# A squared-ReLU MLP on TensorE: the up projection of parts two to four as seven half-size products per tile pair

## The chip, the cores and the metric

The kernel runs on one core of a Trainium2 chip. The metric is the device time of one execution in microseconds. Three runs of the kernel before took 1084.81 to 1085.42 us, median 1085.13. A separate profiled execution took 1085.44 us, of which 1083.7 us lie between its first and its last instruction (the span).

## The reference, cut to what matters

One layer of a hybrid encoder on 512 tokens of width 1024, in float32: a combined input projection, a bidirectional state-space branch, a windowed attention branch, a gated merge and an output projection, then the channel mixing that this change is about:

```python
h = rmsnorm(x, pre_mlp_norm)                       # 512 x 1024
f = jnp.square(jax.nn.relu(h @ w_mlp_in)) @ w_mlp_out   # 1024 -> 4096 -> 1024
x = x + rmsnorm(f, post_mlp_norm)
```

## The kernel before, in words

**Float32 as two float32r numbers.** TensorE multiplies `float32r` operands. Each operand X is split into a high part (a cast on ACT) and a low part (X minus the high part, on POOL or DVE), and a product is three matmuls into one PSUM bank: high x high, high x low, low x high (`mm3`, lines 404 to 408; all matmuls show as line 398). Weights are the stationary operand in the up projection and the moving one in the down projection.

**Quanta.** The program is a list of quanta: each names the weight chunks that it needs and a function that issues its matmuls. `prefetch` (481) loads chunks ahead on SP's queue into three buffers `wr` (line 453) and splits them into three pairs `wh`, `wl`: ACT casts (473), and the letters of a string say which engine subtracts which piece (477; "pppp" is four quarters on POOL, "v" stands for DVE). A list of actions is placed at quantum numbers (`at`); all that is issued inside `held_back` (1341) may not be put ahead of the TensorE instruction issued last before it.

**The order of the work.** The instructions are not run in the order in which they are written. `Planner` (77) knows a cost per instruction and simulates the engines; each engine takes the ready instruction with the earliest due time, except TensorE, which takes the first ready one in program order. `chain` (498) then fixes one order for each engine, SP's queue of DMA issues included. On the chip each engine runs its list strictly in that order.

**The MLP.** The 4096 hidden columns are four parts of 1024, and a part is eight tiles of 128 columns, taken as four pairs (tile n and tile n + 4). An up quantum (`up_quantum`, 1491) is one such tile: 8 blocks of 128 x 3 matmuls, 512 tokens wide, 24 matmuls into one bank `pp`, then ReLU and square (`up_done`, 1441; ACT line 1446, DVE line 1449). After each second tile `combine` (1457) makes from the pair the token-side operands of the down projection.

The down projection of a part is a 2 x 2 block product of tokens and columns, done in the Winograd form of Strassen's scheme: seven products instead of eight, from four sums of the token-side operand (S1 to S4) and four of the weights (T1 to T4). `down_quanta` (1604) lists them and `fold` (1522) issues them: a quantum is one product, 24 matmuls of 512 columns. The T sums are made on DVE (lines 1536, 1537) from the raw weights `wd`, or, where `staged` is given, read ready from DRAM; the split of a down weight is line 1571 (ACT) and 1575 (POOL, or DVE by `LO_DOWN`). `done` (1616) adds a finished bank to the token accumulators `acc` (1621).

Each down quantum of part p is followed by an up quantum of part p + 1. The first three tiles of the first part are split by token halves (`up_halves`), so that they can begin before all tokens have come through the norm: `flip_h2` (1422) transposes the normed tokens on TensorE and splits them into the tiles `b`, called `h2` in the code. The first use of staged sums is `stage_wo` (1347) with `mix_quanta` (1366), for the output projection ahead of the MLP.

## Time and profile before

| | before |
|---|---|
| median of three runs | 1085.13 us (1084.81 to 1085.42) |
| profiled execution: its time, its span | 1085.44 us, 1083.7 us |
| TensorE matmuls: busy, count | 1073.5 us (99%), 5584 |
| DVE busy | 785.1 us (72%) |
| ACT busy | 654.4 us (60%) |
| POOL busy | 808.1 us (75%) |
| bytes moved by DMA | 152.21 MB |
| TensorE clock granted | 0.997 of full speed |

How to read it: the span is cut by engine. PE is TensorE's matmuls, PEld its weight loads, which overlap the matmuls. Matmul durations in the profile contain their pipelined end, so their mean is longer than their distance; the distance of two matmuls in a stretch without holes is the price. The chain of waits follows the last instruction back to what released it. Waits on an engine that is not on that chain cost nothing by themselves. `L1536` in a row is line 1536 of the kernel, and `wt<-wd,wd` are its output and inputs by the program's names.

### The profile page before, as it was taken

Reading aid. Unit: us, or ns where it says so; the run is one execution under the profiler, and the core shown is the slowest. Engines: PE = TensorE matmul, PEld = TensorE weight load, DVE = VectorE, ACT = ScalarE, POOL = GpSimd, SP = SyncE. Lnnn points to the kernel's source line nnn. Section 1 sums busy time; section 2 is a strip of 40 time slices with the busy share of each in tenths; the row PEclk is TensorE's granted clock in tenths of the full one; section 3 lists DMA queues with packets and bytes.
Section 4 is the critical chain, followed back from the end, with each engine's and each line's share of the span. In section 5 each row is a group of like instructions: output and inputs, shape, how many; then the busy total and the mean of one; then the engine's idle time right before and its main releaser. Section 6 shows DMA issues by size and latency. Waiting matters only on the chain.

```text
span 1083.7 us, 16956 instructions
## 1 busy us (share of the span) xinstructions
PE 1073.5 (99%) x5584; PEld 902.2 (83%) x5584; DVE 785.1 (72%) x1345; ACT 654.4 (60%) x1407; POOL 808.1 (75%) x1011
## 2 busy tenths in 40 slices
PE   9999999999999999999999999999999999999997
PEld 8888888888888888888888888889888888888885
DVE  6578787788796787887877558668873755755787
ACT  5566776686865767676686522476755434434443
POOL 4446567557558898989898768566998978978844
PEclk9999999999999999999999999999999999999999
DMA  7444624625536555556564389754722612611522
GB/s 218 118 121 125 150 76 123 146 74 158 131 107 164 149 144 160 158 143 167 136 179 113 103 253 332 226 198 127 237 65 59 201 53 59 198 55 59 161 93 78
DMA packets 221000, 152.21 MB, mean 140 GB/s; under 512 B 12493, under 2 KB 194229, under 8 KB 220912
## 3 DMA queue, kind: packets, MB, share of 16 engines
q1 hardware_dynamic: 220764, 151.06, 48.6%
q8 instruction: 44, 0.72, 0.3%
q14 instruction: 44, 0.36, 0.1%
q10 hardware_dynamic: 148, 0.07, 0.0%
HBM read 138.19 MB, written 12.91 MB: 139 GB/s over the span
## 4 chain that ended last, share of the span: by engine, by line
PE 94%; DVE 2%; DMA 2%; ACT 1%; SPq 1%; issue 1%; POOL 0%; POOLq 0%; DVEq 0%
PE pp L398 66%; PE ps L398 25%; PE ps L402 3%; DMA x<-in_x 1%; DMA wr<-in_w_in 0%; ACT b L423 0%; DVE B L944 0%; DVE x L1401 0%; DVE P L855 0%; DVE x L1655 0%; DVE acc L1621 0%; SPq L383 0%; SPq L570 0%; DVE Q L832 0%; DVE ag L1648 0%
## 5 line engine op out<-in xcount | busy, mean ns | idle before, releaser
L398 PE MATMUL pp<-b,wh 128*128 128x512 f32 (+1 forms) x1840 | 564.8, 388 | 0.2 <-DVE b L424 0.2
L477 POOL TENSOR_TENSOR wl<-wr,wh 128x256 fp32r<-128x256 f32 (+1 forms) x503 | 418.2, 860 | 137.4 <-ACT wh L473 133.9
L398 PEld LDWEIGHTS pp<-b,wh 128*128 128x128 f32 x1840 | 340.2, 188 | 68.2 <-issue 1.5
L398 PE MATMUL pp<-b,wl 128*128 128x512 f32 (+1 forms) x920 | 356.5, 388 | 0.0
L398 PEld LDWEIGHTS pp<-b,wl 128*128 128x128 f32 x920 | 172.9, 188 | 34.3
L473 ACT CAST wh<-wr 128x1024 fp32r<-128x1024 f32 x131 | 136.5, 1042 | 82.0 <-PE pp L398 56.1
L1575 POOL TENSOR_TENSOR wl<-wd,wh 128x256 fp32r<-128x256 f32 x168 | 139.8, 862 | 39.9 <-ACT wh L1571 31.9
L1571 ACT CAST wh<-wd 128x512 fp32r<-128x512 f32 x108 | 63.2, 618 | 53.9 <-PE pp L398 23.8
L398 PE MATMUL ps<-wh,fh 128*128 128x512 f32 (+1 forms) x196 | 75.5, 385 | 0.5 <-DVE acc L1621 0.5
L398 PE MATMUL ps<-wl,fh 128*128 128x512 f32 (+1 forms) x196 | 75.5, 385 | 0.0
L398 PE MATMUL ps<-wh,fl 128*128 128x512 f32 (+1 forms) x196 | 75.4, 385 | 0.0
L1112 ACT ACTIVATE n<-cb,tables 128x128 f32<-128x128 f32 x128 | 48.8, 391 | 26.8 <-DVE cb L1103 22.8
L1449 DVE SCALAR_TENSOR_TENSOR pp<-pp,r 128x512 f32<-128x512 f32 (+1 forms) x31 | 17.5, 565 | 54.0 <-ACT r L1446 53.9
L1575 POOL TENSOR_TENSOR wl<-wt,wh 128x256 fp32r<-128x256 f32 x56 | 45.4, 844 | 9.9 <-ACT wh L1571 6.0
L944 DVE SCALAR_TENSOR_TENSOR u<-pp,cv,u 128x510 f32<-128x510 f32 (+1 forms) x64 | 47.6, 744 | 2.9 <-ACT u L940 1.7
L1042 POOL TENSOR_TENSOR xd<-x,tables 128x256 f32<-128x256 f32 x48 | 35.0, 747 | 19.5 <-ACT x L967 16.9
L1113 ACT ACTIVATE m<-cb,tables 128x128 f32<-128x128 f32 x128 | 48.7, 389 | 0.3 <-DVE cb L1103 0.3
L1148 POOL TENSOR_TENSOR w<-w,E 128x256 f32<-128x256 f32 x48 | 40.3, 852 | 11.1 <-DVE w L1144 5.4
L398 PEld LDWEIGHTS ps<-wh,fh 128*128 128x128 f32 x196 | 36.8, 188 | 8.1 <-DVE acc L1621 0.7
L1108 ACT ACTIVATE rf<-rf,tables 128x128 f32<-128x128 f32 x128 | 41.9, 393 | 2.6 <-DMA rf<-csT 2.6
L398 PEld LDWEIGHTS ps<-wl,fh 128*128 128x128 f32 x196 | 36.8, 188 | 7.4
L398 PEld LDWEIGHTS ps<-wh,fl 128*128 128x128 f32 x196 | 36.8, 188 | 7.2
(301 smaller groups left out, 2085.3 us busy)
## 6 DMA issues: line engine op xcount, KB each, us to landing
wr<-in_w_in SPq DMA_DIRECT2D x74, 512.0 KB, 4.8
wr<-in_w_mlp_in SPq DMA_DIRECT2D x32, 512.0 KB, 4.1
wd<-in_w_mlp_out SPq DMA_DIRECT2D x64, 256.0 KB, 4.7
rb<-csT SPq DMA_DIRECT2D x32, 256.0 KB, 3.9
rf<-csT SPq DMA_DIRECT2D x32, 256.0 KB, 5.5
wr<-in_w_ssd_out SPq DMA_DIRECT2D x14, 512.0 KB, 5.4
wd<-in_w_o SPq DMA_DIRECT2D x28, 256.0 KB, 4.6
E<-csE SPq DMA_DIRECT2D x96, 64.0 KB, 3.9
```

The lines of the kernel that those rows point to most:

```text
L398: self.nc.tensor.matmul(out, lhsT, rhs, start=start, stop=stop, skip_group_check=more)
L402: self.nc.tensor.transpose(out, src, self.ident[:n, :n])
L473: self.nc.scalar.copy(hi[:, :m], raw)
L477: engines[e].tensor_tensor(lo[:, c], raw[:, c], hi[:, c].bitcast(F32), op=ALU.subtract)
L944: nc.vector.scalar_tensor_tensor(u[:, a:e], ps[:, a + d:e + d], self.wtap(t, b), u[:, a:e], op0=ALU.mult, op1=ALU.add)
L1042: nc.gpsimd.tensor_tensor(v4(xd[:, d * 256:(d + 1) * 256]), v4(xs(c)), by_dir(self.coef, c)[:, d].unsqueeze(2).to_broadcast([128, 4, 64]), ...
L1108: nc.scalar.activation(v4(rf)[:, h], v4(rf)[:, h], AF.Identity, bias=ncs[:, 0, h:h + 1])
L1112: nc.scalar.activation(v4(n)[:, h], cb[:, 0], AF.Copy, scale=dt[:, 0, h:h + 1])
L1113: nc.scalar.activation(v4(m)[:, h], cb[:, 1], AF.Copy, scale=dt[:, 1, h:h + 1])
L1148: nc.gpsimd.tensor_tensor(wc, wc, E[:, d], op=ALU.add)
L1571: nc.scalar.copy(hi, w)
L1575: (nc.vector if e == "v" else nc.gpsimd).tensor_tensor(low[:, q], w[:, q], hi[:, q].bitcast(F32), op=ALU.subtract)
```

## The change

The up projection of parts two to four takes the same seven-product form. Its 2 x 2 blocks are halves of the input width (512 rows of `w_mlp_in`), halves of a part's columns, and halves of the tokens (256). For a tile pair there are seven products of 4 blocks x 3 matmuls, 256 tokens wide, in four quanta of two products, the last of one (`one`, `two`, `three`, `four`); they are accumulated in the halves of two banks, X and V in one, Z and Y in the other. ACT copies intermediate banks out (`copy`), DVE adds them back (`plus`), and ReLU and square go by quarters (`square`, which takes the minimum side where a block is held with its sign turned). Part one keeps the old form.

The token-side sums T1 to T4 are made once, after the tokens have been transposed: `flip_h2` also writes a float32 copy of them (`b32`, 16 more ACT operations), `token_sums` makes T1, T2, T4 on DVE with their splits, and `third_sum` splits T3 at the start of part one's down projection.

The weight-side sums S1 to S4 of parts two to four are made by DMA alone, in DRAM: a copy on SP's queue, then an accumulating DMA issued by POOL (`sums_in_dram`), eight transfers of 512 x 512 for each part, at quanta 10, 26 and 42 with two quanta between. In the same way the down sums T1 to T4 of parts three and four are made from 4 and 30 quanta after the start of the up projection on, three quanta between, and read as staged. [...]

A tile pair needs 3.5 chunks of 1024 weight columns instead of 2. Two quarters of each full chunk are subtracted on DVE ("vvpp"), the half chunk on POOL. A quarter of the down splits of parts two and three moves from POOL to DVE ("pppv"). The planner learns costs for DMAs issued by POOL, and counts other transfers as 1.6 times as long while one of them runs. The slots of SBUF grow from 67 to 73, and the scratch for POOL's DMAs is set to 4096.

```diff
-SLOTS, RAW, SPL, PP, AHEAD, SPARE = 67, 3, 3, 3, 4, 6
+SLOTS, RAW, SPL, PP, AHEAD, SPARE = 73, 3, 3, 3, 4, 6
+UP_LO = "vvpp", "vvpp", "vvpp", "pp"
-LO_DOWN = "p", "p", "p", "vp"
+LO_DOWN = "p", "pppv","pppv","vp"
+SOFT, SLOW = 125, 1.6
-FETCH, STAGE = 2, 1
+FETCH, STAGE, HALF = 2, 1, 3
+SUMS = dict(up={1: (10, 2), 2: (26, 2), 3: (42, 2)}, down={2:(104,3),3:(130,3)})
...
             if e == "SP":
-                queue = max(queue, t + self.LEAD) + self.transfer(n)
+                queue = max(queue, t + self.LEAD)
+                queue += self.transfer(n) * (SLOW if queue < soft else 1)
...
+            elif e == "POOL" and "DMA" in type(self.ins[n]).__name__:
+                size = 4 * math.prod(d[1] for d in self.operands(self.ins[n].outs)[0].ap)
+                soft = max(soft, end + self.LEAD) + size / SOFT
+                free[e], end = end, soft + self.TAIL
...
+    def sums_in_dram(self, name, src, q, pace):
+        nc = self.nc
+        t = [self.dp.tile([512, 512], F32, name=f"{name}s{i}") for i in range(1, 5)]
+        def step(out, a, plus):
+            def run():
+                a_ = t[a] if isinstance(a, int) else src(*a)
+                if plus:
+                    nc.gpsimd.dma_start(t[out], a_, accum_op=ALU.add)
+                else:
+                    nc.sync.dma_start(t[out], a_)
+            return run
+        steps = [(0, (0, 0), False), (0, (0, 1), True), (2, (0, 1), False), (2, (1, 1), True),
+                 (1, 0, False), (1, (1, 1), True), (3, 1, False), (3, (1, 0), True)]
+        for i, args in enumerate(steps):
+            self.at(q + pace * i, lambda fn=step(*args): self.held_back(fn))
+        return t
...
+                if t2 == 0:
+                    self.b32.append(self.slots.get("b32"))
+                nc.scalar.activation(self.b32[k + i][:, tok], ps[:, i * 256:(i + 1) * 256], AF.Copy, scale=self.g3(k + i))
...
+    def token_sums(self):
...
+        for k in range(4):
+            b1, b2 = self.b32[k], self.b32[4 + k]
...
+            tt(u[:, lo], b1[:, lo], b1[:, hi], op=ALU.subtract)
+            stt(u[:, hi], u[:, lo], -1.0, b2[:, hi], op0=ALU.mult, op1=ALU.subtract)
+            self.split(h, l, u)
...
+            tt(self.t3[-1][:, half], b2[:, hi], b1[:, hi], op=ALU.subtract)
+            stt(four[-1][:, half], u[:, hi], -1.0, b2[:, lo], op0=ALU.mult, op1=ALU.subtract)
...
+            if k % 2:
+                h, l = self.twin("t4")
+                self.split(h, l, four[-1])
...
+    def up_unit(self, part, k):
...
+        def product(w, b, at, first):
+            ps, cols = bank[at[0]], at[1]
+            for i in range(4):
+                self.mm3(ps[:, cols], (w[0][:, i], w[1][:, i]), self.bt[b][i], first and i == 0, i == 3, not first)
+        def copy(n, at):
+            made[n] = get(n, (128, 256))
+            nc.scalar.copy(made[n], bank[at[0]][:, at[1]])
+        def plus(at, a, n):
+            nc.vector.tensor_tensor(bank[at[0]][:, at[1]], bank[a[0]][:, a[1]], made[n], op=ALU.add)
+            put(made.pop(n))
+        def square(at, r, side, dst=None):
+            a, cols = bank[at[0]], at[1]
+            nc.scalar.activation(r[:, cols], a[:, cols], AF.Relu, scale=1.0 if side == ALU.max else -1.0)
+            nc.vector.scalar_tensor_tensor((dst or a)[:, cols], a[:, cols], 0.0, r[:, cols], op0=side, op1=ALU.mult)
...
+        X, Y, Z, V = (1, lo), (0, hi), (0, lo), (1, hi)
+        def one(w):
+            bank[1] = self.bank("pp")
+            product(w[0], "B11", X, True)
+            copy("c0", X)
+            bank[0] = self.bank("pp")
+            product(w[1], "T1", Y, True)
+            copy("cy", Y)
+        def two(w):
+            product(w[0], "T2", X, False)
+            copy("c1", X)
+            product(w[1], "B21", Z, False)
+            plus(Z, Z, "c0")
+            made["r"] = get("r")
+            square(Z, made["r"], ALU.max)
+            self.operand(part, k, bank[0][:, lo])
+        def three(w):
+            product(w[0], "T3", X, False)
+            plus(V, X, "cy")
+            square(V, get("q"), ALU.min)
+            product(w[1], "B22", Y, False)
+            plus(Y, Y, "c1")
+            square(Y, made["r"], ALU.max, made["r"])
+        def four(w):
+            product(w[0], "T4", X, False)
+            square(X, get("q"), ALU.min)
+            self.pair = [bank[0][:, lo], made["r"][:, hi], made["r"], bank[1]]
+            self.combine(part, k, -1.0)
...
+        return [quantum(("A11", "S1"), one, UP_LO[0]), quantum(("S2", "A12"), two, UP_LO[1]),
+                quantum(("S3", "S4"), three, UP_LO[2]), quantum(("A22",), four, UP_LO[3])]
...
+            if part == 0:
+                self.at(n(), self.third_sum)
+            up = [u for k in range(4) for u in self.up_unit(part + 1, k)] if part < 3 else []
             for i in range(8):
-                self.add(*down[i:i + 1], *([self.up_quantum(8 * part + 8 + i)] if part < 3 else []))
+                self.add(*down[i:i + 1], *up[2 * i:2 * i + 2])
```

So after each of the first seven down quanta two of a pair's four quanta follow, and after the seventh the last two follow directly on the two before them.

177 lines of the change are left out of this document (137 added, 40 removed).

## The prediction

> **What bounds the kernel now.** First the page, then the chain of waits, the waits of TensorE and of the SP queue, and the busy times of stages.
>
> ```profile
> span 1083.7 us, 16956 instructions
> PE 1073.5 (99%) x5584; PEld 902.2 (83%) x5584; DVE 785.1 (72%) x1345; ACT 654.4 (60%) x1407; POOL 808.1 (75%) x1011
> ```
>
> A TensorE that is busy for 99% may still have slack inside its modelled durations, so the pitch of its matmuls is read from the chain (start us, us, what):
>
> ```profile
> 757.96 4.80 PE pp L398 x40
> 762.76 2.40 PE ps L398 x20
> 765.16 21.79 PE pp L398 x96
> 787.40 5.44 PE pp L398 x24
> ...
> 797.83 5.44 PE pp L398 x24
> 803.27 5.44 PE ps L398 x24
> ...
> 1026.31 10.88 PE pp L398 x48
> 1037.19 32.65 PE ps L398 x144
> ```
>
> From 765 us on the pieces follow each other without a hole: 24 matmuls of 512 columns take 5.44 us, 226.7 ns each. The 60 before them belong to the split first tiles, 256 columns wide: 4.80 + 2.40 = 7.20 us, 120.0 ns each. So half the width costs 53% of the full width here, and the weight load that goes with each matmul does not show at that pitch.
>
> ```profile
> PE ps L398 <- DVE acc L1621: 0.5, 1, 0.5
> PE pp L398 <- DVE b L424: 0.2, 1, 0.2
> ```
>
> Those are TensorE's waits outside the start. TensorE alone sets the time, and only fewer matmul nanoseconds, or a new wait, can change it. How near the others are to becoming the bound is read by stage:
>
> ```profile
> core 0: us, PE busy (x) PEld busy (x) DVE busy (x) ACT busy (x) POOL busy (x), PEclk, DMA share, GB/s
> 766.00:787.40 21.40, 21.40 (x96) 17.74 (x95) 17.84 (x36) 14.23 (x31) 21.08 (x33) 1.00 0.82 252
> 787.40:795.00 7.60, 7.60 (x36) 6.28 (x35) 6.50 (x9) 4.02 (x8) 7.60 (x9) 1.00 0.04 13
> 795.00:805.00 10.00, 10.00 (x46) 8.29 (x45) 8.87 (x12) 5.17 (x9) 9.70 (x18) 1.00 0.19 54
> 787.40:869.00 81.60, 81.60 (x362) 67.60 (x361) 49.59 (x75) 41.61 (x74) 75.87 (x102) 1.00 0.35 105
> 869.00:950.60 81.60, 81.60 (x362) 67.59 (x361) 49.17 (x78) 37.18 (x65) 70.64 (x90) 1.00 0.35 104
> 950.60:1037.20 86.60, 86.60 (x384) 71.74 (x383) 54.23 (x88) 38.67 (x69) 69.01 (x85) 1.00 0.29 89
> 200.00:300.00 100.00, 100.00 (x617) 84.91 (x616) 78.98 (x170) 73.54 (x184) 63.63 (x83) 1.00 0.48 125
> ```
>
> The rows from 787.4 on are the stages in which down part one, two, three runs with up part two, three, four between. POOL is the second bound (93% in the first of them), DVE has some 30 us of room in each, but almost none between 766 and 805.
>
> **The change part by part.** *TensorE.* A tile pair of parts two to four was 48 matmuls of 512 columns, 2 x 5.44 = 10.88 us; it becomes 7 products x 4 blocks x 3 = 84 of 256 columns, 84 x 120.0 ns = 10.08 us. Twelve pairs x 0.80 = **9.60 us removed**. Nothing else on TensorE changes.
>
> *Bank hand-overs inside a pair.* Seven products share two PSUM banks, and copies, additions and squares lie between them. The costs:
>
> ```profile
> L415 ACT CAST fh<-pp 128x256 fp32r<-128x256 f32 x8 | 3.0, 373 | 7.2 <-DVE r L1449 4.7 <-DVE pp L1449 2.6
> L1449 DVE SCALAR_TENSOR_TENSOR pp<-pp,r 128x256 f32<-128x256 f32 x4 | 1.7, 425 | 6.2 <-ACT r L1446 6.2
> L1449 DVE SCALAR_TENSOR_TENSOR pp<-pp,r 128x512 f32<-128x512 f32 x4 | 2.8, 696 | 11.9 <-ACT r L1446 11.9
> ```
>
> Before the last product (T4) the third (T3) must be added and squared: addition 0.42, relu 0.37, square 0.43 = 1.22 us, under the B22 product, 12 x 120 ns = 1.44 us. That leaves 0.22 us for three semaphore hand-overs, so some wait is likely there unless a down product is put in between. Between the second and third quantum of a pair a down product (5.44 us) covers the longer chain (2.0 us), except in the fourth pair of each part, where no down product is left. Bounds: 0, or 12 x 0.2 + 3 x 1.2 = 6.0 us. A planner that puts the first matmuls of the next ready product there removes most of it; I take 1.0.
>
> *Splits of weights.* 3.5 chunks of 1024 columns per pair instead of 2. POOL keeps its eight quarter pieces per pair; the six new ones go to DVE, and ACT casts 1.5 chunks more.
>
> ```profile
> L477 POOL TENSOR_TENSOR wl<-wr,wh x503: 713/742/2408, 21.6 to 1024.7; 128x256 fp32r<-128x256 f32 x167, 128x1024 fp32r<-128x1024 f32 x1
> L477 DVE TENSOR_TENSOR wl<-wr,wh x6: 410/950/964, 740.9 to 745.7; 128x256 fp32r<-128x256 f32 x6
> L477 DVE TENSOR_TENSOR wl<-wr,wh 128x256 fp32r<-128x256 f32 x6 | 4.3, 774 | 0.0
> L1575 DVE TENSOR_TENSOR wl<-wd,wh x24: 679/692/1232, 669.2 to 1065.0; 128x512 fp32r<-128x512 f32 x24
> L416 DVE TENSOR_TENSOR fl<-fs,fh x16: 682/993/1359, 770.3 to 1042.6; 128x512 fp32r<-128x512 f32 x16
> L473 ACT CAST wh<-wr 128x1024 fp32r<-128x1024 f32 x8 | 8.4, 1051 | 8.1 <-PE pp L398 6.5 <-DMA wd<-in_w_mlp_out 0.7 <-PE ps L398 0.3
> ```
>
> The second row is the price that decides: the same DVE subtraction takes 0.41 us or 0.95 us. The short ones fall where POOL is pausing, the long ones beside POOL's subtractions. The Trainium skill ("SBUF — State Buffer", section "Who interferes with whom" and its practical consequences) says that a DVE instruction with two SBUF inputs and a GpSimd instruction that reads SBUF block each other for the whole instruction. The two values of the row agree with it; by that rule nearly all the new splits would cost the long price, which is the second rival below.
>
> ACT gets per part at most 4 x (1.5 x 1.05 + 3 copies x 0.37 + 4 relus x 0.37) = 17 us on 37 to 42 of 78: nothing, covered by its idle time; without that cover DVE, which waits for each cast, would be late by as much. DVE per part: 24 d for the splits (d between 0.41 and 0.95), 8 additions x 0.42 = 3.4, and 16 squares of 0.425 for 4 x 0.70 + 8 x 0.425, 0.6 more. A quarter of the down splits of parts two and three also moves to it, 7 x 0.83 = 5.8 us a part (bounds 0.68 to 1.23).
>
> *Token sums.* Per block pair four operations of 256 columns and one split subtraction of 512, and two more splits per four: 4 x (4 x 0.41 + 0.68) + 2 x 0.68 = 10.6 us of DVE, or at the long prices 4 x (4 x 0.95 + 1.36) + 2 x 1.36 = 23.4; I take 15. They are wanted from 794 us on. From 766 to 805 DVE is idle 3.6 + 1.1 + 1.1 = 5.8 us. So some 9 us are pushed behind 805 us; what is late next is the down weights' sums on DVE, operands of products that TensorE wants in the same stretch. Bounds: 0 (later DVE work gives way, as after 805 the first stage is only 61% busy), or the full 9; I take 2.0.
>
> *Stages one and two as a whole.* DVE needs 49.6 + 49.2 + 48 d + 2 x 4.0 + 5.8 + 2.0 (the third token sum) + 7 carried over = 121.6 + 48 d, and TensorE would leave 2 x 78.4 = 156.8 us. DVE is the bound above d = 0.73. I take d = 0.74, near the mean of the six rows (0.77), as POOL works less in the second stage (14 pieces x 0.83 = 11.6 us less): 0.3 us, and 1.0 for queueing of an engine that is then 100% planned. In stage three the staged down sums remove 16 sums from DVE,
>
> ```profile
> L1536 DVE TENSOR_TENSOR wt<-wd,wd 128x512 f32<-128x512 f32 x8 | 8.0, 996 | 1.5 <-POOL wl L1575 0.8 <-DMA wd<-in_w_mlp_out 0.7
> L1536 DVE TENSOR_TENSOR wd<-wd,wd 128x512 f32<-128x512 f32 x4 | 4.6, 1158 | 5.8 <-DMA wd<-in_w_mlp_out 5.8
> L1537 DVE TENSOR_TENSOR wd<-wd,wd 128x512 f32<-128x512 f32 x4 | 4.4, 1096 | 0.0
> ```
>
> 17.0 us, so its full 3.2 us arrives. That relief itself gains nothing, since TensorE waits for nothing there now.
>
> *Sums in DRAM.* Five sets of eight 1 MB transfers: 20 copies on SP's queue, 20 accumulating ones issued by POOL, and 15 MB more weight loads.
>
> ```profile
> q1 hardware_dynamic: 220764, 151.06, 48.6%
> wr<-in_w_mlp_in SPq DMA_DIRECT2D x32, 512.0 KB, 4.1
> wot<-wd SPq DMA_DIRECT2D x16, 256.0 KB, 4.7
> SPq L453 <- POOL wl L477: 261.5, 96, 7.2
> ```
>
> No row shows an accumulating transfer. At the queue's own rate (151 MB in 48.6% of 1083.7 us, 287 GB/s) 1 MB takes 3.7 us; reading twice and writing once, three times that, 11 us. Three sets run up to quantum 57, about the first 330 us at 5.4 us a quantum and a little more, where the DMA engines are 48% busy and POOL 64%; two run from the up projection on. A weight load is issued as soon as POOL frees its buffer, three buffers deep, about two quanta (10.9 us) before it is wanted, and takes 4.1: some 6.8 us late is free. A single transfer of 3.7 to 11 us ahead of it is thus hidden or nearly so. The Trainium skill ("DMA: Bandwidth & Descriptors", "Anatomy of one DMA") gives a GpSimd-issued transfer about 2.0 us plus bytes over 436 GB/s, an estimate of 4.4 us for 1 MB, and the sum would be the same. POOL's own issue cost is bounded by its shortest and longest work rows, 0.2 and 2.4 us; eight fall where POOL would be at 75.9 of 78.4, yet they can slide into the second stage, as their readers come later still. Bounds 0 and 4; I take 0.8 for all of this.
>
> **Sum**, on the profiled execution's 1085.44 us: -9.6 + 1.0 + 2.0 + 1.3 + 0.8 = -4.5, 1080.9. It stood 0.3 above the median of the runs, so **1080.6 us**.
>
> **The rivals.** (1) *All cover holds*: the planner's order hides every hand-over; -9.6, with 0.6 of unavoidable edges: 1076. For it: today TensorE waits 0.7 us in the whole second half though POOL is 93% busy. Against: DVE's 766 to 805. (2) *DVE becomes the bound*: every new split costs 0.95 beside POOL, and the seven moved ones 1.23 (2.8 more): 121.6 + 45.6 + 2.8 = 170.0 against 156.8, 13.2 lost for 9.6 won, +3.6: 1088.7. It eats the whole gain from d = 0.93. For it: four of the six rows are at 0.95. Against: the 512-wide splits of the down weights have median 0.69. (3) *SP's queue stands behind a sum*: in each set two copies read an accumulated block, so SP waits for POOL's transfer, and every weight load stands behind it. The copy comes three steps (33 us) after the accumulation. If that takes 45 us (a twelfth of the rate above), each blocks 12 us, 5.2 more than a load can be late: ten copies, +52 less 9.6, 1127. Against: that is four times the upper bound. (4) *The hand-overs cost their upper bound*, 6.0 instead of 1.0, because the order finds nothing to put between: 1085.6, no change. Against: the planner puts the first ready matmul next. (5) *It does not do what it says*: a 256-column stream paced by its weight loads. The rows at 120.0 ns exclude all but 1%.
>
> **How the numbers follow.** Forecast (1078 to 1083) 0.42, (1) 0.22, (4) 0.13, (2) 0.15, (3) with (5) 0.08. About 0.2% (2.2 us) is what a measurement of this kernel can tell from no change: faster, below 1083, is the forecast, (1) and the near edge of (4), 0.66; within 0.2% most of (4) and the near edge of (2), 0.13; slower the rest, 0.21. The range 1075.3 to 1089 takes in (1) and most of (2); (3) and the far end of (2) stay out.
>
> **What would show it.** The chain should still be TensorE's, a pair of parts two to four taking 10.1 us and a stage 78.4 to 80. The new DVE splits should have a mean near 0.74; above 0.93 the second rival holds. TensorE's waits should name DVE between 790 and 830 us, and the PSUM operations of the pairs. SP's waits should name no accumulating transfer for more than 7 us. I am wrong if stage three too is over 80 us, or if TensorE waits in the first 600 us.

## The result, and the profile after

The changed kernel takes 1102.73 us (median of 4 runs, 1099.62 to 1104.93) against 1085.28 us for the kernel before beside it. The ratio is 1.0157, 95% interval 1.0129 to 1.0185: 1.6% slower, where 1080.6 us had been predicted, with a range up to 1089.0.

The page of the changed kernel: engines, the two large DMA queues, and the chain that ended last.

```profile
span 1101.6 us, 18311 instructions
PE 1074.3 (98%) x6016; PEld 915.6 (83%) x6016; DVE 838.7 (76%) x1471; ACT 695.3 (63%) x1515; POOL 814.4 (74%) x1003
...
q1 hardware_dynamic: 249212, 187.77, 58.5%
q0 software_dynamic: 10560, 20.97, 11.6%
...
PE 61%; DVE 9%; DMA 3%; ACT 3%; issue 2%; SPq 1%; POOL 0%; POOLq 0%; DVEq 0%; ACTq 0%
```

TensorE now holds only 61% of the chain. The new queue q0 holds the accumulating transfers: 20.97 MB, whose packets took 11.6% of the time of 16 DMA engines over 1101.6 us. For each of the 20 transfers that is 127.8 / 20 = 6.4 us of all 16 engines, added up over the engines; it does not show that all were busy with it at once.

To see where the time went, both executions are cut at the same piece of work, ahead of the last 1316 matmuls before and the last 1750 after (the difference is the 432 that the change adds). The first part reaches into the up projection of part one, the second holds the down stages with the new products. Stretches, before and then after; columns: us, busy us and count of TensorE, weight loads, DVE, ACT, POOL, then clock, DMA share, GB/s.

```profile
0.00:779.80 779.80, 777.59 (x4270) 656.91 (x4271) 587.96 (x1029) 514.35 (x1153) 563.98 (x704) 1.00 0.56 157
779.80:1076.00 296.20, 295.69 (x1316) 245.24 (x1314) 193.35 (x310) 139.52 (x252) 243.10 (x307) 1.00 0.32 96
```

```profile
0.00:790.90 790.90, 780.91 (x4268) 656.02 (x4269) 589.93 (x1036) 519.38 (x1170) 575.47 (x713) 1.00 0.70 186
790.90:1093.90 303.00, 293.19 (x1750) 259.60 (x1748) 245.02 (x428) 175.36 (x343) 237.99 (x290) 0.99 0.73 203
```

The first part, in which TensorE's work is unchanged, is **11.1 us later**. The second takes 303.0 us. With the predicted 9.6 us less work it would take 296.2 - 9.6 = 286.6 if nothing new were waited for, so **16.4 us are lost in it**. The sum, 11.1 - 9.6 + 16.4 = 17.9, is the difference of the spans, 1101.6 - 1083.7. Not all of it is seen as waiting. Idle time of TensorE (length less busy time) is 7.8 us more than before in the first part and 9.3 more in the second; the rest, 3.3 and 7.1 us, lies in matmuls that took longer than before or than priced. A slower clock after a wait is one cause (0.73 in a row below); holes that the modelled durations hide are another, since the timeline gives 0.39 us to a matmul of 512 columns whose pitch is 0.227.

The saving itself is there, by a row of the chain (start us, us, what):

```profile
1002.87 5.75 PE pp L412 x48
```

48 half-width matmuls take 5.75 us, 119.8 ns each, as priced. TensorE's longest waits (us in all, times, longest):

```profile
PE ps L416 <- DVE P L893: 5.0, 4, 3.3
PE pp L412 <- DVE fal L430: 2.5, 3, 1.2
PE pp L412 <- DVE pp L1573: 2.2, 2, 1.2
```

The first is in the scan steps, far ahead of the new products, and the kernel before does not have it: `P` are attention weights, which DVE makes in one queue with the scan's row blocks. The three stages, each from the first matmul of a part's down products to that of the next part's:

```profile
803.80:885.10 81.30, 78.69 (x481) 70.54 (x480) 70.93 (x110) 50.26 (x95) 72.50 (x87) 0.98 0.64 179
885.10:969.10 84.00, 80.78 (x506) 71.55 (x505) 69.62 (x125) 47.13 (x92) 69.59 (x81) 1.00 0.94 242
969.10:1051.90 82.80, 79.38 (x506) 71.78 (x505) 59.60 (x112) 49.64 (x97) 60.22 (x74) 1.00 0.69 204
```

The stages take 81.3, 84.0 and 82.8 us instead of 78.4. The first holds 24 up matmuls fewer than the others, which run behind its end.

**The scan steps.** Stretches at TensorE's largest hole in the first half:

```profile
290.00:300.00 10.00, 9.36 (x43) 7.41 (x41) 2.08 (x3) 6.18 (x21) 2.27 (x3) 1.00 0.77 169
300.00:310.00 10.00, 5.84 (x21) 4.22 (x22) 9.96 (x23) 6.86 (x16) 8.37 (x10) 0.73 0.59 193
```

The issue of an accumulating transfer on POOL and then of a row block `rf` of the scan on SP (start us, us of issue), and that of the row block in the kernel before:

```profile
278.91 0.99 POOL L1460 DMA_DIRECT2D up2s<-in_w_mlp_in  x1
...
284.14 1.66 SPq L1110 DMA_DIRECT2D rf<-csT  x1
```

```profile
289.57 0.55 SPq L1087 DMA_DIRECT2D rf<-csT  x1
```

The row block is issued 5.2 us behind the accumulating transfer, in 1.66 us instead of 0.55, and its landing is then on the chain:

```profile
284.14 9.66 DMA rf<-csT
```

Over all 32 of these loads the median to landing rose from 5.5 to 6.8 us. DVE starves first (2.08 of 10 us busy from 290), then TensorE waits for it. The accumulating transfers' issue on POOL (ns: min, median, max; first and last start) and their us to landing:

```profile
L1460 POOL DMA_DIRECT2D up2s<-in_w_mlp_in x4: 989/1033/1113, 215.0 to 324.8; - x4
...
DMA to landing us min/median/max: 10.0/11.8/13.6
```

1 MB lands after 11.8 us. By the Trainium skill ("DMA: Bandwidth & Descriptors", "Anatomy of one DMA") 4.4 us had been estimated for it; here the measurement decides.

**The stages.** A stretch of the timeline, ACT and then TensorE (start us, us, instruction, in brackets the idle time before it and what ended it):

```profile
991.40 0.62 ACT L1766 CAST wh<-wd 128x512 fp32r<-128x512 f32 x1 [5.72 <-DMA wd<-dn2s]
991.92 0.36 ACT L429 CAST fah<-pp 128x256 fp32r<-128x256 f32 x1
...
992.80 0.51 PE L412 MATMUL pp<-b,wh 128*128 128x256 f32 x2 [1.18 <-DVE fal L430]
```

A late load of a staged block (5.72 us) passes through ACT's queue, in which the cast of `fa` stands behind it, and DVE's split into TensorE. Three late loads of down weights are on the chain of the stages:

```profile
916.02 8.10 DMA wd<-in_w_mlp_out
961.79 7.10 DMA wd<-dn2s
981.89 10.78 DMA wd<-dn2s
```

The first and the third are followed on the chain, through the queues of DVE and ACT, by the addition and the square ahead of a T4 product, at 932.04 and 995.94. These are TensorE's two waits for the square (2.2 us above); so the waits look like bank hand-overs and begin with a load. In the middle stage the DMA engines are busy for a share of 0.94. The group of the new DVE splits from 780 us on (count, us in all, mean ns):

```profile
L500 DVE TENSOR_TENSOR wl<-wr,wh 128x256 fp32r<-128x256 f32 x72 | 53.0, 749 | 9.2 <-ACT wh L492 8.8 <-DMA wd<-in_w_mlp_out 0.3
```

And one of them in the timeline, DVE and then POOL:

```profile
868.55 5.38 DVE L500 TENSOR_TENSOR wl<-wr,wh 128x256 fp32r<-128x256 f32 x1 [0.65 <-ACT wh L492]
873.85 0.41 DVE L1573 SCALAR_TENSOR_TENSOR r<-pp,r 128x256 f32<-128x256 f32 x1
...
865.25 5.62 POOL L1770 TENSOR_TENSOR wl<-wd,wh 128x256 fp32r<-128x256 f32 x8
870.82 2.83 POOL L500 TENSOR_TENSOR wl<-wr,wh 128x256 fp32r<-128x256 f32 x4
```

A subtraction of 0.41 us takes 5.38: it ends 0.28 us after the last of twelve POOL subtractions that follow each other without a gap (870.82 + 2.83 = 873.65). It had started 3.3 us into the first eight, so at 5.62 / 8 = 0.70 us each some eight of them ran while it was held. The bank's square at 873.85 stood behind it.

### The profile page after: what moved, and what is told of

Read it like the earlier page. It is cut to its first block, busy times and chain, and to the rows that moved or that the text cites. A ratio compares the mean times of both kernels' runs of the same rounds, so it can differ in the third digit from the quotient of the medians.

```text
span 1101.6 us, 18311 instructions
## 1 busy us (share of the span) xinstructions
PE 1074.3 (98%) x6016; PEld 915.6 (83%) x6016; DVE 838.7 (76%) x1471; ACT 695.3 (63%) x1515; POOL 814.4 (74%) x1003
## 3 DMA queue, kind: packets, MB, share of 16 engines
q0 software_dynamic: 10560, 20.97, 11.6%
## 4 chain that ended last, share of the span: by engine, by line
PE 61%; DVE 9%; DMA 3%; ACT 3%; issue 2%; SPq 1%; POOL 0%; POOLq 0%; DVEq 0%; ACTq 0%
PE pp L412 44%; PE ps L412 16%; DMA wd<-dn2s 2%; DVE wd L1729 1%; DMA rf<-csT 1%; PE ps L416 1%; DVE wl L500 1%; DMA wd<-in_w_mlp_out 1%; DVE fsl L430 1%; DVE acc L1816 1%; ACT P L887 0%; DVE wt L1728 0%; DVE ftl L430 0%; ACT m L1136 0%; DVE P L893 0%
## 5 line engine op out<-in xcount | busy, mean ns | idle before, releaser
L412 PE MATMUL pp<-b,wh 128*128 128x512 f32 (+1 forms) x1840 | 519.3, 366 | 4.7 <-DVE fal L430 2.5
L492 ACT CAST wh<-wr 128x1024 fp32r<-128x1024 f32 (+1 forms) x155 | 156.5, 1009 | 80.6 <-PE pp L412 46.6
L500 DVE TENSOR_TENSOR wl<-wr,wh 128x256 fp32r<-128x256 f32 x78 | 56.8, 744 | 9.4 <-ACT wh L492 9.1
L967 DVE SCALAR_TENSOR_TENSOR u<-pp,cv,u 128x510 f32<-128x510 f32 (+1 forms) x64 | 47.7, 746 | 13.3 <-ACT u L963 11.9
L887 ACT ACTIVATE P<-P,mx 128x384 f32<-128x384 f32 (+1 forms) x64 | 35.2, 552 | 13.8 <-DVE mx L884 13.8
L1129 POOL TENSOR_TENSOR rb<-rb,tables 128x512 f32<-128x512 f32 x32 | 34.2, 1075 | 12.0 <-DMA rb<-csT 8.6
L1816 DVE TENSOR_TENSOR acc<-acc,ps 128x512 f32<-128x512 f32 (+1 forms) x49 | 32.6, 668 | 12.2 <-PE ps L412 12.2
L878 DVE CUSTOM_DVE_ANT_0 P<-ps,bt,sink 128x256 f32<-128x256 f32 (+1 forms) x64 | 31.9, 545 | 10.4 <-PE ps L412 9.9
L1770 DVE TENSOR_TENSOR wl<-wd,wh 128x512 fp32r<-128x512 f32 x40 | 31.6, 797 | 10.3 <-ACT wh L1766 9.2
L1095 POOL TENSOR_TENSOR pv<-pv,tables 128x256 f32<-128x256 f32 x32 | 24.5, 778 | 16.6 <-DVE pv L1096 10.3
L1132 DVE TENSOR_TENSOR rf<-rf,rb 128x512 f32<-128x512 f32 x32 | 31.0, 970 | 4.4 <-POOL rb L1129 4.4
```

What stands on the lines that cost most here:

```text
L412: self.nc.tensor.matmul(out, lhsT, rhs, start=start, stop=stop, skip_group_check=more)
L492: self.nc.scalar.copy(hi[:, :m], raw)
L500: engines[e].tensor_tensor(lo[:, c], raw[:, c], hi[:, c].bitcast(F32), op=ALU.subtract)
L887: nc.scalar.activation(p[:, :w], p[:, :w], AF.Exp, bias=mx[:, n:n + 1], accum_out=sm[:, n:n + 1])
L967: nc.vector.scalar_tensor_tensor(u[:, a:e], ps[:, a + d:e + d], self.wtap(t, b), u[:, a:e], op0=ALU.mult, op1=ALU.add)
L1770: (nc.vector if e == "v" else nc.gpsimd).tensor_tensor(low[:, q], w[:, q], hi[:, q].bitcast(F32), op=ALU.subtract)
```

## The experiments

In the table "first" is how much later than before the first part ends, "lost" the second part's length over 286.6 us (over 296.2 with the old products, 293.0 with four new pairs). Both are of the profiled execution, whose time stands beside them; it can lie several us off the median, so a loss holds for that execution.

| kernel | median us | ratio to before (95%) | profiled us | first | lost |
|---|---|---|---|---|---|
| changed | 1102.73 | 1.0157 (1.0129 to 1.0185) | 1103.85 | +11.1 | 16.4 |
| no_sums | 1086.37 | 1.0022 (0.9999 to 1.0046) | 1082.60 | 0.0 | 6.8 |
| sums_alone | 1098.53 | 1.0123 (1.0108 to 1.0138) | 1099.76 | +14.1 | 0.1 |
| lows_on_act | 1102.45 | 1.0170 (1.0133 to 1.0208) | 1104.02 | +14.3 | 13.8 |
| no_token_sums | 1109.26 | 1.0220 (1.0205 to 1.0236) | 1107.08 | +8.5 | 22.7 |
| no_sums_act_lows | 1083.82 | 0.9987 (0.9965 to 1.0008) | 1086.93 | +1.4 | 9.7 |
| sums_copies_only | 1085.12 | 0.9998 (0.9989 to 1.0008) | 1085.16 | +0.1 | 0.1 |
| part_four_only | 1085.98 | 1.0011 (0.9999 to 1.0022) | 1089.96 | -0.4 | 7.6 |
| costed_90_20 | 1097.07 | 1.0109 (1.0092 to 1.0126) | 1095.60 | +2.4 | 17.0 |
| no_up_sums | 1092.09 | 1.0069 (1.0047 to 1.0092) | 1092.09 | +2.2 | 13.8 |
| no_down_sums | 1095.09 | 1.0101 (1.0058 to 1.0145) | 1095.07 | +14.2 | 4.9 |
| no_sums_pool_zeros | 1082.72 | 0.9974 (0.9963 to 0.9985) | 1082.94 | +1.2 | 6.4 |
| down_sums_early | 1112.04 | 1.0222 (1.0188 to 1.0256) | 1114.85 | +25.2 | 13.3 |
| alone_quarters | 1118.14 | 1.0300 (1.0263 to 1.0337) | 1117.07 | not read | not read |
| no_v_square | 1081.63 | 0.9961 (0.9949 to 0.9973) | 1083.43 | +1.5 | 6.6 |
| costed_halves | 1094.15 | 1.0075 (1.0050 to 1.0101) | 1092.70 | +2.3 | 14.5 |
| part_four_halves | 1095.11 | 1.0081 (1.0055 to 1.0107) | 1089.02 | -0.8 | 7.1 |

Every edit also changes the order that the planner writes, so 2 or 3 us between two rows prove nothing by themselves.

### Without the sums, and the sums alone

no_sums:

```diff
-src.update(zip(("S1", "S2", "S3", "S4"), self.sums_in_dram(f"up{part}", ...)))
+src.update(S1=src["A22"], S2=src["A21"], S3=src["A11"], S4=src["A12"])
-return dict(zip(("T1", "T2", "T3", "T4"), self.sums_in_dram(f"dn{part}", half, q, pace)))
+return {"T1": half(0, 0), "T2": half(0, 1), "T3": half(1, 0), "T4": half(1, 1)}
```

> The sums in DRAM are left out: the up units read blocks of the weights themselves in place of S1 to S4, and down parts three and four read blocks in place of T1 to T4, with as many loads as the changed kernel. No accumulating DMA and no 1 MB copy is left; the output is another. Theory A (the sums' traffic delays the loads that stand beside and behind it): the 10 us lost near 300 us go, and the waits on down weights after 915 us, about 7 us, too: 1085 to 1087. Theory B (DVE, loaded with splits beside POOL, is the bound of the stages; the sums cost only what is seen near 300 us): 1092 to 1094, with the holes between 798 and 1000 us still there. Both as large as the trace suggests: 1086.

sums_alone:

```diff
-self.at(n() + 3, self.token_sums)
...
-up = [u for k in range(4) for u in self.up_unit(part + 1, k)] if part < 3 else []
+up = [self.up_quantum(8 * part + 8 + j) for j in range(8)] if part < 3 else []
```

> The reverse: the up projection of parts two to four goes back to whole tiles, the token sums are left out, and the five sets of sums in DRAM stay (the up sums are made and not read; the down sums are read). It removes all the work that the change puts on DVE and ACT except the moved quarter of the down splits. TensorE has its 9.6 us again. Theory A: 1085.3 plus 10 near 300 us plus some 5 later, 1095 to 1101. Theory B: at most the 10 near 300 us, and if those are an accident of the order, 1085.

Stretches of no_sums, then of sums_alone:

```profile
779.80:1073.20 293.40, 290.29 (x1750) 258.02 (x1748) 240.35 (x428) 175.61 (x343) 233.24 (x283) 1.00 0.51 155
```

```profile
0.00:793.90 793.90, 783.28 (x4269) 658.82 (x4270) 587.04 (x1028) 512.46 (x1153) 576.18 (x714) 0.99 0.70 187
793.90:1090.20 296.30, 295.79 (x1316) 245.26 (x1314) 178.47 (x293) 138.55 (x253) 221.03 (x289) 1.00 0.63 171
```

The sums alone cost 14.1 us in the first part and nothing in the second, although two of the five sets run there. Without them the first part is as before, but 6.8 us stay lost in the second, so not the sums alone are at fault. The runs of no_sums are also spread from 1081.53 to 1093.40, those of the kernel before in the same job from 1084.19 to 1087.05. Its profiled execution is one of the fastest, 3.8 us under the median; by the medians leaving out the sums gains 16.4 us (1102.73 to 1086.37), and some 10.8 us over TensorE's need stay (1.2 + 9.6). Both totals lie where theory A had put them.

The trace of no_sums names what TensorE waited for longest in the second part:

```profile
806.59 0.50 PE L412 MATMUL ps<-wl,fsh 128*128 128x512 f32 x1 [1.31 <-POOL wl L1770]
```

That and one more wait of 0.93 us, at 808.60, are for low parts of down weights, which POOL subtracts. No wait for a bank of the up products is among its waits in this part.

### DVE's share: splits and token sums

lows_on_act:

```diff
-UP_LO = "vvpp", "vvpp", "vvpp", "pp"
+UP_LO = "aapp", "aapp", "aapp", "pp"
+            if e == "a":
+                self.nc.scalar.activation(lo[:, c], raw[:, c], AF.Copy, scale=0.0)
```

> The two quarters of each up chunk that DVE subtracts are instead written as zeros by ACT (the low parts of half the up weights are left out, so the output is less exact). DVE loses 72 subtractions of about 0.9 us; ACT gets 72 activations of about 0.4. All transfers stay. Theory B: the holes between 798 and 1000 us close, 17 us: 1085 to 1088. Theory A: little changes, 1098 to 1103.

no_token_sums (the products with T read blocks of the tokens):

```diff
-        self.at(n() + 3, self.token_sums)
+        self.at(n() + 3, self.token_blocks)
```

> The token sums and their float32 copies are left out (blocks of the tokens stand in for T1 to T4, so the output is another); all else stays. DVE loses about 15 us of work between 770 and 830 us, ACT about 11. Theory B: the first stage's backlog goes, the holes at 815 to 830 us and part of those at 870 to 890 us close: 3 to 6 us, 1097 to 1100. Theory A: no change, 1102 to 1103.

Neither made the kernel faster than the changed one: 1102.45 lies where theory A had put it, 1109.26 above both expectations. With DVE's 72 splits gone 13.8 us stay lost in the second part instead of 16.4. Without the token sums 22.7 are lost: more, though DVE has less to do. In that trace four DVE splits took 2.2 to 3.4 us, and TensorE waited 5.7 us in three waits for ACT's copies out of the banks and 4.1 us once for a DVE split; why that order is worse stays open. DVE's amount of work alone is not what decides.

no_sums_act_lows joins no_sums and lows_on_act:

> The changed kernel without its sums in DRAM (the four source blocks stand in for the sums, so the products of S and T use wrong operands and 40 transfers of 1 MB are left out) and, besides, without the 72 low-part subtractions that DVE makes for the new up weights (ACT writes zeros in their place, so half of the up weights of parts two to four have no low part). Asked: why the version without sums was still at 1086 us, about 8 us above what TensorE's shorter products alone would give. If DVE, taken up by the splits beside GpSimd's, is what holds TensorE in the two stages: 72 x 0.69 = 50 us less DVE work, the holes of about 8 us close and the time is 1076 to 1080 us. If the bank hand-overs inside a pair are the cause, which both versions share: 1083 to 1088 us, as without sums alone.

Its ten runs fall into two groups, 1079.52 to 1081.42 and 1086.23 to 1088.50, five each. The profiled one is of the second group. Its timeline, DVE, POOL and TensorE:

```profile
841.07 7.10 DVE L430 TENSOR_TENSOR fsl<-fs,fsh 128x512 fp32r<-128x512 f32 x1
...
842.05 5.57 POOL L1773 TENSOR_TENSOR wl<-wd,wh 128x256 fp32r<-128x256 f32 x8
...
849.75 0.58 PE L412 MATMUL pp<-t12h,wh 128*128 128x256 f32 x1 [4.74 <-ACT c L1567]
```

The stretch after TensorE's wait, of the same kernel:

```profile
850.00:852.50 2.50, 2.50 (x13) 2.50 (x14) 0.00 (x0) 1.23 (x2) 1.42 (x2) 0.50 0.02 7
```

One DVE subtraction of 0.69 us took 7.10, until POOL's run ended (842.05 + 5.57 = 847.62). A cast on ACT waited for the next one, the copies out of the banks stood behind the cast, TensorE waited 4.74 us and then ran at a granted clock of 0.50, 13 matmuls in 2.5 us where 120 ns each would make 21. That is 4.74 + 1.25, some 6 us, near the distance of the groups (medians 1080.25 and 1086.93). That the faster group is the one without such an event is likely but not shown: only one of the ten has a profile. The median, 1083.82, lies between the groups and settles neither expectation.

### Copies or accumulations

sums_copies_only, from sums_alone:

```diff
-                if plus:
-                    nc.gpsimd.dma_start(t[out], a_, accum_op=ALU.add)
-                else:
+                if not plus:
                     nc.sync.dma_start(t[out], a_)
```

> The old whole-tile up projection with the five sets of sums beside it, of which only the 20 plain copies on SP's queue remain; the 20 accumulating transfers of GpSimd are left out, so the staged blocks of the down weights are not sums. With all 40 the same kernel took 1098.5 us, 13 over the kernel before. If the accumulating transfers (11 to 12.5 us each, and 1 us of GpSimd's time) make the loss: 1085 to 1088 us. If the plain copies on the queue of the loads make it (20 MB in 1 MB pieces ahead of loads that are wanted within 10 us): 1094 to 1098 us. If both by their bytes (a copy reads and writes 2 MB, an accumulation 3 MB): 1090 to 1092 us.

```profile
0.00:779.90 779.90, 777.71 (x4269) 656.23 (x4270) 586.97 (x1028) 513.35 (x1153) 564.68 (x702) 1.00 0.61 175
```

The 20 copies on SP's own queue cost nothing; with the 20 accumulating transfers, and the order that the planner writes for them, come the whole 14.1 us.

### Order, place and size of the accumulating transfers

costed_90_20 lets the planner reckon 1 MB at 90 bytes a ns, 11.7 us and near the measured 11.8, instead of 8.4, and a load beside it at twice its time instead of 1.6 times:

```diff
-SOFT, SLOW = 125, 1.6
+SOFT, SLOW = 90, 2.0
```

> The changed kernel with other costs in its planner: a transfer counts double instead of 1.6-fold beside an accumulation, for 90 instead of 125 us of the planner's time; the same instructions in another order. If the loss is an order that reckons the sums too cheap: 1090 to 1096 us. If it is the traffic itself, which no order takes away: 1099 to 1106 us, as the changed kernel.

```profile
0.00:782.20 782.20, 778.88 (x4268) 656.52 (x4269) 595.27 (x1036) 520.18 (x1170) 579.67 (x713) 1.00 0.71 188
782.20:1085.80 303.60, 294.34 (x1750) 260.89 (x1748) 249.10 (x428) 175.87 (x343) 240.11 (x290) 0.99 0.73 203
```

With the same transfers in the first part (71% DMA share against 70%) only 2.4 us of the 11.1 are left: the traffic fits, and the order of the changed kernel had no room for its real duration. At the place shown above the new order issues the row block at 279.95 and the accumulating transfer behind it, at 287.25. Two prices were changed together, so which of them matters is not shown. The second part gains nothing by it. The time lies between the two expectations.

no_up_sums and no_down_sums each make one of the two replacements shown for no_sums:

> The changed kernel with the three sets of sums of the up weights left out (blocks stand in for them), the two sets of the down weights kept. TensorE's need in the stages is the same. If the loss splits into about 10 us by the up sums in the first half and about 10 by the down sums beside the new up products (the changed kernel lost 16.6 us after 791 us, the one without any sums 6.8): 1085.4 - 9.6 + 16 = 1090 to 1094 us, and nothing lost before 640 us. If the down sums are as harmless here as they were beside whole-tile up products: 1083 to 1087 us.

> The changed kernel with the two sets of sums of the down weights left out (blocks stand in for them), the three sets of the up weights kept. By the same split: 8 to 10 us lost before 640 us, and 7 lost after, as in the kernel without any sums: 1085.4 - 9.6 + 9 + 7 = 1089 to 1094 us. If the down sums are harmless: 1099 to 1104 us, as the changed kernel.

Stretches of no_up_sums, then of no_down_sums:

```profile
0.00:782.00 782.00, 778.25 (x4268) 655.59 (x4269) 589.53 (x1036) 520.18 (x1170) 564.25 (x701) 1.00 0.56 156
782.00:1082.40 300.40, 292.01 (x1750) 258.31 (x1748) 239.25 (x429) 175.21 (x343) 239.85 (x290) 1.00 0.74 205
```

```profile
0.00:794.00 794.00, 783.29 (x4267) 657.96 (x4268) 589.71 (x1036) 519.64 (x1170) 577.02 (x712) 0.99 0.69 184
794.00:1085.50 291.50, 290.05 (x1750) 257.87 (x1748) 243.64 (x428) 176.47 (x343) 232.51 (x283) 1.00 0.51 156
```

The loss splits by part. The up sums cost the first part 9 us when they are left out of the changed kernel (11.1 against 2.2) and 14 when they are added to the kernel without sums (14.2 against 0.0). The down sums cost the second part 7 to 11.5 us by the same two comparisons (13.8 against 6.8, 16.4 against 4.9), although the same two sets cost 0.1 beside whole-tile up products. By the medians leaving out the up sums gains 10.6 us and the down sums 7.6. 1092.09 lies inside the first expectation of no_up_sums, 1095.09 just above that of no_down_sums. Some 5 to 7 us of the second part belong to neither. In no_down_sums TensorE's waits there come to 1.3 us, none longer than 0.6; its busy time is 290.05 us where 295.69 - 9.6 = 286.1 would do, so most of that loss is spread over the stages in pieces too short to be named.

down_sums_early is costed_90_20 with the down sums at quanta 58 and 74:

```diff
-SUMS = dict(up={...}, down={2:(104,3),3:(130,3)})
+SUMS = dict(up={...}, down={2: (58, 2), 3: (74, 2)})
```

> The changed kernel with the dearer costs in its planner (double for 90 us, where it took 1097.1 us and lost nothing before 640 us) and with the two sets of down sums moved from the MLP stages to the scan steps behind the up sums (from quantum 58 and 74). Complete computation. If the accumulations next to the MLP's weight loads are what costs there, the MLP goes back to the 7 us of the version without sums, and if the scan steps take two more sets without loss: 1083 to 1088 us. If the scan steps cannot take them, the loss moves there: 1095 to 1105 us.

The first part is 25.2 us late, some 14 of it coming between 600 and 660 us, where the DMA engines are busy for a share of 1.00. Two more sets do not fit into these steps in this order, and 13.3 us stay lost in the second part, where one DVE split was again held 5.4 us.

alone_quarters cuts each accumulation of sums_alone into four:

```diff
+                    p = slice(j * (512 // 4), (j + 1) * (512 // 4))
-                    nc.gpsimd.dma_start(t[out], a_, accum_op=ALU.add)
+                    nc.gpsimd.dma_start(t[out][p], a_[p], accum_op=ALU.add)
```

> The old whole-tile up projection with the five sets of sums beside it (1098.5 us with 1 MB accumulating transfers, all of it lost before 320 us), each accumulating transfer cut into four of 256 KB that are spread over the same two quanta. If loads suffer because they stand behind one long burst of 11 to 12.5 us: 1086 to 1090 us. If it is the bytes, which are the same: 1095 to 1100 us. If each piece costs as much as a whole one: over 1110 us.

Its total says nothing about the question: the planner put 16 of the 32 pieces of the down sums behind the down products (issued from 1085 to 1104 us), so these read unfinished blocks and the end is some 28 us longer. The first 600 us can be read. There TensorE is 5.1 us behind the kernel before (its first 3384 matmuls are issued by 605.1 us instead of 600.0), 4.5 us of it lost between 200 and 250 us; sums_alone is 14.5 us behind at the same matmul (614.5). By 330 us two of the three up sets had been issued in both, so the same bytes in pieces that land after a median of 6.7 to 6.9 us cost about a third. This does not show more than costed_90_20 did, since the planner also orders by the pieces.

costed_halves is costed_90_20 with each accumulation cut in two:

> The changed kernel, complete, with the dearer costs in its planner (1097.1 us) and every accumulating transfer cut in two of 512 KB. If bursts are the cost in the MLP stages: 1087 to 1092 us. If the bytes are: 1095 to 1099 us. Below 1083 us it would beat the kernel before.

14.5 us stay lost in the second part instead of 17.0, no more than another order alone can make. The time, 1094.15, lies between the two expectations, so neither is confirmed.

### What is lost without any sums

no_sums_pool_zeros, from no_sums:

```diff
+            if e == "p" and self.low_zero:
+                nc0.memset(lo[:, c].bitcast(F32), 0.0)
+                continue
             engines[e].tensor_tensor(lo[:, c], raw[:, c], hi[:, c].bitcast(F32), op=ALU.subtract)
```

> The version without any sums in DRAM in which, from the MLP on, GpSimd also writes zeros into the low parts of its weight pieces instead of subtracting (it reads no SBUF; the low parts of those weights are left out). DVE keeps all its work. Asked: whether the spread of the version without sums (1081.5 to 1093.4 us) and its last 7 us come from DVE instructions with two SBUF inputs that are held while GpSimd's subtractions follow each other without a gap (one was held 7.1 us, and TensorE then waited 4.7). If so: no DVE instruction over 2 us, 1076 to 1079 us, and a spread under 3 us. If the holes come from the bank hand-overs, or from loads: 1082 to 1088 us, or the same spread.

The 72 new splits from 780 us on in this kernel:

```profile
L504 DVE TENSOR_TENSOR wl<-wr,wh 128x256 fp32r<-128x256 f32 x72 | 28.4, 420 | 20.4 <-PE pp L412 10.5 <-ACT wh L492 7.2 <-POOL wl L502 1.4
```

A bank hand-over in its timeline (ACT, DVE, TensorE):

```profile
855.64 0.62 ACT L1770 CAST wh<-wd 128x512 fp32r<-128x512 f32 x1 [2.89 <-PE pp L412]
856.16 0.38 ACT L1576 ACTIVATE q<-pp 128x256 f32<-128x256 f32 x1
...
856.57 0.43 DVE L1577 SCALAR_TENSOR_TENSOR pp<-pp,q 128x256 f32<-128x256 f32 x1 [1.79 <-ACT q L1576]
...
857.06 0.38 PE L412 MATMUL pp<-t4h,wh 128*128 128x256 f32 x1 [1.08 <-DVE pp L1577]
```

Two of the three things expected held, the time did not. The spread shrinks to 2.7 us (1081.24 to 1083.98), no DVE instruction of the stages is held, and a split takes 420 ns where the changed kernel's same 72 took 749. The Trainium skill ("SBUF — State Buffer", "Who interferes with whom") says that a DVE instruction with two SBUF inputs meets only a GpSimd instruction that reads SBUF, not one that only writes it; the 420 ns agree. The median falls from 1086.37 to 1082.72, so that interference was worth some 4 us without sums. But 6.4 us stay lost. The rows show one of the places: the addition of the block was done at 854.78, yet its relu on ACT ran at 856.16, behind a cast of down weights that itself waited for a buffer that TensorE had to free. T4 followed at 857.06. Four such holes ahead of T4 come to 3.4 us in this trace. The trace of no_sums, with POOL subtracting, has no wait ahead of T4, so these holes are not what was lost there.

no_v_square, from no_sums_pool_zeros:

```diff
             plus(V, X, "cy")
-            square(V, get("q"), ALU.min)
```

> The version without sums in DRAM and with zeros from GpSimd (1082.7 us; TensorE waited 3.4 us in four places ahead of the T4 product) in which the relu and square of the fourth block of each pair are left out too, so that T4 waits for the addition alone. If the last 6 us are bank hand-overs: these four waits go and the time is 1078.5 to 1080.5 us. If the waits stand for something else (loads, DVE as such): 1082 to 1083.5 us.

Neither expectation. The time is 1.1 us lower, 1081.63 (1079.27 to 1083.43), and in the profiled execution, the slowest of its ten, 6.6 us are still lost, but at another place. DVE and TensorE there:

```profile
871.15 0.69 DVE L1732 TENSOR_TENSOR wd<-wd,wd 128x512 f32<-128x512 f32 x1 [3.11 <-DMA wd<-in_w_mlp_out]
...
873.03 0.42 DVE L1571 TENSOR_TENSOR pp<-pp,cy 128x256 f32<-128x256 f32 x1
...
873.51 0.40 PE L412 MATMUL pp<-t4h,wh 128*128 128x256 f32 x1 [2.75 <-DVE pp L1571]
```

Now T4 waits for the addition, which stands on DVE behind a sum of down weights whose load is 3.11 us late. What the two traces have in common is not the square but an instruction in ACT's or DVE's fixed order that waits for something else and stands between two products of one bank.

### Is there a version that beats both?

part_four_only keeps whole tiles in parts two and three, has one set of up sums, and makes the token sums later:

```diff
-LO_DOWN = "p", "pppv","pppv","vp"
-SUMS = dict(up={1: (10, 2), 2: (26, 2), 3: (42, 2)}, down={2:(104,3),3:(130,3)})
+LO_DOWN = "p", "p", "p", "vp"
+SUMS = dict(up={3: (42, 2)}, down={2: (104, 3), 3: (130, 3)})
```

> Seven half-size products only in the up projection of part four, whole tiles in parts two and three; one set of up sums (from quantum 42 on, in the stretch where the changed kernel showed no further shift) and the two sets of down sums as in the changed kernel; the token sums are made in the third stage from the split tokens. Complete computation. TensorE loses 4 x 0.80 = 3.2 us. If the loss came from the two sets of up sums that run beside the first scan steps (up to about 330 us): 1081 to 1084 us, faster than the kernel before. If one set of up sums beside scan steps costs as much as the others: 1085 to 1089 us. If the down sums cost more than that in the last two stages: 1088 to 1092 us.

part_four_halves adds the planner's dearer costs and halved accumulations to it:

> The version with seven products in part four alone (1086.0 us), complete, with the dearer costs in the planner and every accumulating transfer cut in two. TensorE has 3.2 us less to do than before. If order and bursts were what ate it: 1082 to 1084 us. If DVE instructions held up by GpSimd and the hand-overs ate it: 1085 to 1088 us.

No. The first is equal to the kernel before (1085.98, 1084.85 to 1089.96), the second slower (1095.11, 1089.02 to 1099.94). The saving is 3.2 us. The profiled execution of the first is the slowest of its ten, 4.0 us over the median, that of the second the fastest of its eight, 6.1 under; so the 7.6 and 7.1 us lost in their second parts are neither of them typical. Most of the first one's loss lies at one place in stage one, whose up products are still whole tiles:

```profile
860.24 0.50 PE L413 MATMUL ps<-wh,f12h 128*128 128x512 f32 x1 [1.53 <-ACT wh L1765]
862.12 0.50 PE L413 MATMUL ps<-wl,f12h 128*128 128x512 f32 x1 [1.38 <-POOL wl L1769]
```

TensorE waits there for the split of a down weight. Ahead of it DVE had two instructions held, 7.74 us at 817.50 and 6.24 at 840.90; that they made the split late is not shown, and sums_alone had one held 7.45 us in that stage and lost 0.1 us.

No complete version that was run beats the kernel before.

## Why the prediction was wrong, step by step

*TensorE, -9.6: right.* 119.8 ns a matmul against 120.0. The 432 matmuls more and the half width came out at the price that the first tiles had shown.

*Sums in DRAM, 0.8 with bounds 0 and 4: the step that failed.* It measured 9 to 14 us in the first part (up sums) and 7 to 11.5 in the second (down sums); by the medians leaving out all of them gains 16.4 us. The duration was a little outside the bounds of the prediction, 3.7 to 11: 11.8 us to landing (10.0 to 13.6). POOL's issue is 1.0 us, inside 0.2 to 2.4. What was wrong above all was the cover. The 6.8 us of slack were those of a weight load, three buffers ahead. The row blocks of the scan (`rf`, `rb`, `E`) share SP's queue with the weights, and the one at 284.14 had no such slack: its landing is on the chain. The sentence "a single transfer of 3.7 to 11 us ahead of it is thus hidden or nearly so" never looked at them, though 48% DMA share was read from the page as if it were room for a burst. The planner made the same error with a price of 8.4 us; with 11.7 us, and a doubled price for loads beside a transfer, most of the loss in the first part went.

*Down sums as a relief.* They were said to gain nothing and to let stage three keep its full 3.2 us. In fact their accumulations fall into stages that load 75% more up weights than before (3.5 chunks per pair instead of 2), with a DMA share of 0.94 in the middle one, and staged blocks come late (7.10 and 10.78 us on the chain). That this traffic makes them late fits the rows and no_down_sums, where the share of the second part falls from 0.73 to 0.51; which transfer delays which was not isolated. The sign by which the prediction was to fail, a third stage over 80 us, is there: 82.8.

*Hand-overs, 1.0 with bounds 0 and 6.0: inside the bounds, for another reason.* In the changed kernel TensorE waits 2.2 us for the square ahead of T4 and 1.6 for a copy out of a bank, 3.8 in all. The reckoning had the chain run as soon as its operands were there (1.22 us under 1.44) and missed that it stands in ACT's and DVE's queues behind instructions that wait for something else, here late loads. The 5 to 7 us that stay lost without any sums are not explained by this term: no_sums waits for POOL's splits and for no bank of the up products, and only with POOL writing zeros do holes ahead of T4 appear, 3.4 of 6.4 us. What the rest is stays open.

*DVE.* The price of a new split was right: d = 0.74 against 0.749 measured, and the second rival (0.95 each) did not happen. But the mean hides the rare one that is held for 5 us, which no term had. DVE was not the bound that the sum made of it (157.1 us of work for 156.8): it is busy for 70.93 + 69.62 = 140.6 us of the first two stages, which take 165.3. The crowding by the token sums is there, DVE being busy for 43.00 of the 43.40 us from 779.8 to 823.2, but TensorE is idle for only 0.85 us of them. The price of 2.0 was not shown; leaving the token sums out gave a slower kernel.

*The rivals.* None had the result. The third named the right resource, SP's queue and the accumulating transfers, by the wrong mechanism: no wait of SP names one of them among its twelve largest, and its 1127 us rested on 45 us a transfer. "TensorE waits in the first 600 us" was named as a sign of being wrong, and it was the first one to be seen.

## What to carry to other kernels

Slack has to be read for the most urgent transfer that shares the DMA engines, not for the one that the change adds; a mean DMA share of 48% did not cover transfers that took 11.8 us to land. Splitting a product into more and shorter ones puts more short instructions of other engines between TensorE's instructions, and each of them can inherit a stall of the queue in which it stands: a late load, a cast without a buffer, a held subtraction. Where an order is planned from prices, measure a new operation once and give the planner that price before judging the change.

## What the runs showed of the hardware that was not expected

- An accumulating DRAM-to-DRAM transfer of 1 MB lands after 10.0 to 13.6 us and takes 6.4 us of all 16 DMA engines' time, added up; pieces of 256 KB land after medians of 6.7 to 8.7 us.
- Behind one, issuing a 256 KB load on SP took 1.66 us instead of 0.55 (one pair of rows).
- A DVE subtraction with two SBUF inputs beside POOL's subtractions takes longer (749 against 420 ns on average), which fits waiting for one of them, but now and then it is held for the rest of a whole run, some eight of 0.70 us in the row above: 5.38, 7.10 and 7.74 us. With POOL only writing, none was over 1 us in the stages. In the trace of the kernel before the longest in the stages was 3.35 us. What decides between the two was not found.
- After a wait of 4.74 us the granted clock was 0.50 for about 2.5 us, 13 matmuls instead of 21; after the waits around 303 us of the changed kernel the mean of ten microseconds was 0.73.
